# A hybrid decoder layer on one core: TensorE's order planned by another rule, true transposes, paired doubling, and two column groups at the end

## The chip, the cores and the metric

The kernel runs on one core of one Trainium2 chip. The metric is the device time of one execution in microseconds (us); lower is better. Engines are called as the profile calls them: PE is TensorE (PEld its weight loads), DVE is VectorE, ACT is ScalarE, POOL is GpSimd, SP is SyncE, which here only issues DMAs.

## What is computed

One layer over 560 tokens (16 learned tokens and 512 of a prompt in one sequence, 32 of eight short sequences), width 1024, all in fp32:

```python
h = rms_norm(x, g_mix)
proj = h @ w_in
glu_a, glu_b, qkv, z, b_raw, a_raw, gate_c, gate_d = jnp.split(proj, cuts, axis=-1)
c = jax.nn.silu(layer_norm(depthwise31(glu_a * sigmoid(glu_b)) + b_dw, ln_g, ln_b))
q, k, v = jnp.split(jax.nn.silu(depthwise4(qkv)), 3, axis=-1)    # heads of 128, q and k l2-normalised
g = -jnp.exp(a_log) * softplus(a_raw + dt_bias)                  # decay per token and head
o, S_new = gated_delta(q, k, v, sigmoid(b_raw), g, S0)           # 8 heads
o = rms_norm(o, g_head) * jax.nn.silu(z)
x = x + (sigmoid(gate_c) * (c @ w_cout) + sigmoid(gate_d) * (o @ w_dout)) @ w_o
x = x + jnp.square(jax.nn.relu(rms_norm(x, g_mlp) @ w_up)) @ w_down
y = rms_norm(x, g_final)
```

The gated delta rule is evaluated in chunks: within a chunk a triangular system is solved, and the state S (128x128 per head) is carried from chunk to chunk, S <- decay * S + k^T u, with o = (q S) * decay + (masked q k^T) u.

## The kernel before, in words

Every large matrix product is made of three products of rounded parts: weight high part by input high part, weight high by input low, weight low by input high. `gemm` goes through 88 chunks of weights (1024 x 128 each), called by their index here: 0 to 7 are those of k, 64 to 71 those of gate_c, 80 to 87 those of w_o. A chunk takes 48 matmuls at L613, called mains: for each of 8 input slices two with the high and two with the low input part (mains 0 to 31 of the chunk), and then 16 with the weight's low part. Below, mains are numbered from the first of chunk 0, so that chunk 3 is mains 144 to 191. Chunks 0 to 3 (NRAW = 4) run on the input before its norm, whose high parts lie in the tiles V2 to V9, one for each slice, and whose low parts lie in RT; chunks from 4 on run on the normalised h in tile R1. After `gemm` comes the MLP (L2083 up, L2234 down), whose matmuls are mains too.

Between the mains stand small matmuls of other streams:

- `g_stage` makes the decays: L681, L685 and L687 on PE, exponentials on ACT, then two products on POOL (L706, tiles zs0 and zs1), which PE reads in L710, L711 and L712.
- `d_gm` makes for each of the 8 heads two products on POOL (L739, a 128x512 mask times the decays). They are written to V4 to V9 in turn, three heads in six tiles, so the first six of them overwrite what the mains of chunk 3 read. `d_stage` reads them on PE (L755 to L760).
- `doubling` (L1108, L1119: 64 matmuls of 64x64) is the last step of the triangular solve.
- `head_prep` turns v, k and q of a head's short sequences (L1411, L1413, L1415, L1419) and its k (L1452), and makes the masked q k^T (L1469). `chain` walks a head's chunks: L1503 reads the state, L1518 makes u, L1522 and L1525 use it, L1537 copies o on ACT. `decode_state` writes the states of the short sequences, `head_post` norms o (L1660, L1669).
- The end: `ev_part` adds the last product to x, `mean_of` sums the squares of a group of token columns (L2282), `fin_part` adds eps (L2334, DVE), takes the power -0.5 (L2336, POOL), broadcasts it (L2340, PE), scales (L2350, L2346, DVE) and writes out (L2353). `warm` (L300) issues matmuls whose result nobody reads.

What order all this has is decided when the program is built. `Weaver` is a list scheduler: each stream yields the next operation with its engine, an assumed cost and what it depends on. The scheduler always emits the operation that can start earliest by its own books. Ties go by the stream's priority. The engines then run each its own list in that order, and waits are on semaphores. So a wait at the head of an engine's list holds up everything behind it. One line matters for the prediction: in `d_gm` the start is booked as

```python
t = E("g").t
yield wait(("mm", NRAW - 1))
```

so the books take the time of g alone, and not the end of chunk 3's mains, though the semaphores make POOL wait for the readers of V4 to V9.

## Time and profile before

| | before |
|---|---|
| median of 3 runs | 1069.06 us (1068.16 to 1070.02) |
| the profiled execution's own time | 1068.65 us |
| its span in the profile | 1066.9 us |
| PE busy | 1048.2 us, 98% |
| DVE, ACT, POOL busy | 769.4, 622.9, 148.1 us |

The span is the time between the first and the last instruction of the core; some 1.75 us of the profiled execution's time lie outside it. Busy times of PE are modelled from pipelined matmuls, so the distance from one start to the next is the better measure of what a matmul costs.

### The profile page before, as it was taken

What the parts mean: (1) busy time and instruction counts of PE and PEld (TensorE: products, weight loads), DVE (VectorE), ACT (ScalarE), POOL (GpSimd) and SP (SyncE); (2) the same over time, 40 slices, a digit from 0 to 9 for tenths busy, and PEclk for the clock granted to TensorE, in tenths of its full rate; (3) what the DMA queues carried; (4) which work ended last, traced back from release to release, by engine and by line L of the source; (5) the groups of instructions that cost most, each with busy time, mean ns of one, the idle gap of its engine ahead of it and who ended that gap; (6) DMA issues with size and microseconds to landing.
All of it is one profiled execution on the core that took longest, in us unless ns stands there. A gap on an engine that the chain in (4) does not pass through costs nothing.

```text
span 1066.9 us, 21819 instructions
## 1 busy us (share of the span) xinstructions
PE 1048.2 (98%) x8835; PEld 1026.1 (96%) x8835; DVE 769.4 (72%) x1360; ACT 622.9 (58%) x1285; POOL 148.1 (14%) x173
## 2 busy tenths in 40 slices
PE   8999999999999999999999999999999999999997
PEld 6988999999999999899999999999999999999996
DVE  5888879788889887788953355778657547746754
ACT  5677334668787878776358424578327426723741
POOL 2067311102211221122111000000000000000000
PEclk9999999999999999999999999999999999999998
DMA  6232687467576566667877522654365365346222
GB/s 213 82 89 70 124 178 164 87 148 161 139 172 164 143 137 156 164 166 182 187 163 158 179 84 91 163 153 117 109 177 129 100 153 149 94 124 164 80 61 84
DMA packets 57872, 145.55 MB, mean 136 GB/s; under 512 B 14612, under 2 KB 20140, under 8 KB 57772
## 3 DMA queue, kind: packets, MB, share of 16 engines
q1 hardware_dynamic: 46828, 104.32, 30.4%
q0 software_dynamic: 10944, 39.85, 23.2%
q8 instruction: 69, 1.13, 0.4%
q14 instruction: 31, 0.25, 0.1%
HBM read 135.14 MB, written 9.01 MB: 135 GB/s over the span
## 4 chain that ended last, share of the span: by engine, by line
PE 87%; DVE 5%; ACT 3%; DMA 3%; issue 2%; SPq 0%; POOL 0%; POOLq 0%; DVEq 0%; ACTq 0%
PE pg L613 42%; PE pg L2234 17%; PE bk L2083 15%; DVE acc L815 1%; DMA pre<-in_sq_dram 1%; DVE V L1217 1%; PE pg L2083 1%; PE bk L1419 1%; PE bk L1518 1%; PE bk L978 1%; DVE of L815 1%; PE bk L1522 1%; PE bk L1503 1%; DMA M<-in_xT_dram 1%; PE bk L1525 1%
## 5 line engine op out<-in xcount | busy, mean ns | idle before, releaser
L613 PE MATMUL pg<-R,wh 128*128 128x280 f32 (+2 forms) x1920 | 279.3, 295 | 1.0 <-ACT pre L803 1.0
L613 PEld LDWEIGHTS pg<-R,wh 128*128 128x128 f32 x1920 | 253.7, 189 | 3.9 <-issue 1.5
L1217 DVE SCALAR_TENSOR_TENSOR V<-V,vec,V 128x512 f32<-128x512 f32 x240 | 180.5, 781 | 2.2
L568 ACT ACTIVATE wh<-wraw 128x1024 fp32r<-128x1024 f32 (+1 forms) x89 | 93.4, 1049 | 94.3 <-PE pg L613 79.3
L613 PE MATMUL pg<-R,wl 128*128 128x280 f32 (+2 forms) x960 | 144.0, 294 | 0.3 <-issue 0.3
L613 PEld LDWEIGHTS pg<-R,wl 128*128 128x128 f32 x960 | 128.5, 189 | 1.8 <-issue 1.4
L581 POOL DMA_DIRECT2D wl<-in_w_dram x60 | 52.6, 876 | 343.8 <-ACT wl L579 252.5
L2014 ACT ACTIVATE whm<-RT 128x512 fp32r<-128x512 f32 x73 | 45.2, 625 | 53.0 <-PE pg L2234 34.8
L579 ACT ACTIVATE wl<-wh 128x1024 fp32r<-128x1024 f32 x60 | 63.5, 1058 | 14.8 <-PE pg L613 12.9
L1969 POOL DMA_DIRECT2D RT<-in_wu_dram x16 | 13.8, 865 | 381.6 <-DMA RT<-in_wu_dram 185.6
L2017 DVE TENSOR_TENSOR wlm<-RT,whm 128x512 fp32r<-128x512 f32 x73 | 49.8, 687 | 16.9 <-issue 8.4
L2234 PE MATMUL pg<-RD,whm 128*128 128x272 f32 (+2 forms) x272 | 57.7, 288 | 0.0
L2234 PE MATMUL pg<-K,whm 128*128 128x272 f32 (+2 forms) x272 | 57.6, 288 | 0.0
L2083 PE MATMUL bk<-R,whm 128*128 128x272 f32 x318 | 54.5, 288 | 0.0
L613 PE MATMUL pg<-K,wh 128*128 128x272 f32 x256 | 53.0, 289 | 0.2 <-DVE K L1766 0.2
L613 PE MATMUL pg<-RD,wh 128*128 128x272 f32 x256 | 53.2, 289 | 0.0
L2234 PE MATMUL pg<-RD,M 128*128 128x272 f32 x264 | 46.2, 288 | 0.0
L2014 ACT ACTIVATE whm<-wrawm 128x512 fp32r<-128x512 f32 x43 | 26.7, 623 | 32.6 <-PE pg L2234 29.7
L2083 PEld LDWEIGHTS bk<-R,whm 128*128 128x128 f32 x318 | 45.6, 189 | 0.0
L585 DVE TENSOR_TENSOR wl<-wraw,wh 128x1024 fp32r<-128x1024 f32 x28 | 35.1, 1253 | 13.5 <-ACT wh L568 9.5
L2234 PE MATMUL pg<-RD,wlm 128*128 128x272 f32 (+2 forms) x272 | 43.5, 289 | 0.0
L2234 PEld LDWEIGHTS pg<-K,whm 128*128 128x128 f32 x272 | 43.5, 188 | 0.0
(524 smaller groups left out, 2442.5 us busy)
## 6 DMA issues: line engine op xcount, KB each, us to landing
wraw<-in_w_dram SPq DMA_DIRECT2D x87, 512.0 KB, 3.8
wl<-in_w_dram POOLq DMA_DIRECT2D x60, 512.0 KB, 5.6
RT<-in_wu_dram SPq DMA_DIRECT2D x24, 512.0 KB, 5.2
RT<-in_wu_dram POOLq DMA_DIRECT2D x16, 512.0 KB, 7.3
wrawm<-in_wn_dram SPq DMA_DIRECT2D x16, 512.0 KB, 3.6
RT<-in_wn_dram SPq DMA_DIRECT2D x16, 512.0 KB, 3.5
M<-in_sd_dram SPq DMA_DIRECT2D x16, 256.0 KB, 3.4
out_osd_dram<-M SPq DMA_DIRECT2D x16, 256.0 KB, 3.8
```

The costliest lines, as they stand in the source:

```text
L568: nc.scalar.activation(wh[:, c[0]:c[1]], w[:, c[0]:c[1]], AF.Copy)
L579: nc.scalar.activation(wl, wh.bitcast(F32), AF.Copy, scale=-1.0)
L581: nc.gpsimd.dma_start(wl, i["w"][n].bitcast(F32R), accum_op=ALU.add)
L585: nc.vector.tensor_tensor(wl, w, wh.bitcast(F32), op=ALU.subtract)
L613: nc.tensor.matmul(pt[:, hf, 0:N], w[idx][:, k, :], x[:, off + hf * N:off + hf * N + N], start=k == 0 and not part and x is hi, stop=k == ...
L815: nc.vector.scalar_tensor_tensor(acc[:, 0:584], pr[:, q:q + 584], vcol(w + q), acc[:, 0:584], op0=ALU.mult, op1=ALU.add)
L1217: nc.vector.scalar_tensor_tensor(cc[:, 0:512], G[r][:, 16 + q:528 + q], vcol(w + q), cc[:, 0:512], op0=ALU.mult, op1=ALU.add)
L1969: nc.gpsimd.dma_start(rb, i["wu"][g][:, 1024:2048], accum_op=ALU.add)
L2014: nc.scalar.activation(hi, raw, AF.Copy)
L2017: nc.vector.tensor_tensor(lo, raw, hi.bitcast(F32), op=ALU.subtract)
L2083: nc.tensor.matmul(acc[an], w[:, kp, :], x, start=kp == 0 and not part and x is hi and m not in (3, 6, 7), stop=kp == 3 and part == 1, ski ...
L2234: nc.tensor.matmul(out, w[:, k % 4, :], x[:, a], start=n_ == 0 and x is hi, stop=n_ == len(STEPS) - 1)
```

## The change

The instructions keep their meaning; what changes is order, the form of some small matmuls, and the end. Lines after the change are 9 to 27 higher than before it (L739 is L748, L706 is L715, L710 is L719, L613 is L622, L1108 is L1119, L1119 is L1124, L2350 is L2377).

- The scheduler: an operation on PE is ranked by its start, its priority and its age alone. Mains are marked, and one that follows a small matmul is booked 0.09 us longer. All of PE's order is planned anew by this.
- Low parts of chunks 64 to 71: subtracted on DVE (as for chunks 0 to 11) and no longer by ACT and an accumulating DMA of POOL.
- Doubling: the second half's first step and the first half's second step go in pairs of matmuls on different quarters of the array.
- `head_prep`: v4 and, for seven heads, k4 are turned by PE's transpose and not by a product with the identity; so is o's last slice in `head_post`. The factor s moves from the masked q k^T and from kd into the copy of u on ACT, so the four DVE operations per head that made `at` become one of 128x512, and `sk` is not made. The stream `chain` is started after it.
- `chain`: the two halves of the PSUM bank that hold k S and u change places every other chunk.
- `decode_state` has a higher priority; a reciprocal of the MLP's norm waits for an earlier product.
- The end: the second part's 240 columns are two groups of 120 (before: three of 80); 8 matmuls of `warm` run while POOL takes the power; the scale by g_final of the last slice is done on ACT, so its product is a plain one on DVE; the first part's last three products and their DMAs wait until the second part's eps is added.

```diff
+                if eng == "pe":
+                    key, switch = (start, s[0], s[1]), False
+                    if best is None or key < best[0]:
+                        best = (key, s, eng, start, cost + (0.09 if self.small and tab == "main" else 0.0), tab)
+                    continue
...
-        A0, A1 = 12, 72
+        A0, A1 = 12, 64
...
-            for m in range(32):
-                t = yield op("pe", 0.058, tn[m // 16], tb)
+            def first(m, cost):
+                tb_[m // 8] = yield op("pe", cost, tn[m // 16], tb)
                 nc.tensor.matmul(B[m // 8][64:128, m % 8, :], KT[0:64, m, 64:128], Tn[0:64, m, :], start=True, stop=True)
...
+            def second(m, cost):
+                q = m // 8
+                tb_[q] = yield op("pe", cost, t1[q], *tc_[2 * (m // 16):2 * (m // 16) + 2])
+                nc.tensor.matmul(B[q][0:64, m % 8, :], P2[m // 16][64:128, m % 16, :], CTT[64:128, m, 64:128],
                                  start=True, stop=True)
...
+            for q in (2, 3):
+                for m in range(8 * q, 8 * q + 8):
+                    yield from first(m, 0.07)
+                    yield from second(m - 16, 0.07)
+                yield from keep(q)
+                yield from done(q - 2)
...
-            nc.tensor.matmul(b4[:96, 0:128], M2["v4"], ident, start=True, stop=True)
...
+            nc.tensor.transpose(b4[:96, 0:128], M2["v4"], ident)
+            yield op("pe", 0.12 if wk > 64 else 0.22, tv, tb4)
+            if wk > 64:
+                nc.tensor.transpose(b4[:wk, 128:256], k4, ident)
...
+            nc.vector.tensor_tensor(at, b.rearrange("p (t c) -> p t c", c=128), Ds[hh], op=ALU.mult)
...
+                ba, bu = (bx[:, 256:384], bx[:, 0:128]) if j % 2 else (bx[:, 0:128], bx[:, 256:384])
                 if j:
-                    t = yield op("pe", 0.22, ts, to)
-                    nc.tensor.matmul(bx[:, 0:128], ks, S, start=True, stop=True)
+                    t = yield op("pe", 0.22, ts)
+                    nc.tensor.matmul(ba, ks, S, start=True, stop=True)
...
-                nc.scalar.activation(u, bx[:, 256:384], AF.Copy)
+                nc.scalar.activation(u, bu, AF.Copy, scale=st["s"][:, hh, j:j + 1])
...
-            W.spawn(decode_state(hh, tu), 1)
+            W.spawn(decode_state(hh, tu), -2)
...
-            nc.tensor.matmul(b4[:, 0:48], ob[:, 4, :], ident[:, 0:48], start=True, stop=True)
+            t4 = yield op("pe", 0.12, t1, tb4)
+            nc.tensor.transpose(b4[:, 0:128], ob[:, 4, :], ident)
...
-        NQ = (76, 80)
+        NQ = (76, 120)
...
+            E(("eps", hf)).set(t)
+            if hf:
+                W.spawn(warm(NPOW), -4)
...
+                if c == 5 and hf == 0:
+                    yield wait(("eps", 1))
```

Two places in the new order. The first is POOL's list at the decays, before and after, from the first L739 (now L748) on; V4 to V9, zs0 and zs1 are the tiles written, the second operand gives the decays.

```order
L739 TENSOR_TENSOR V4_89_785<-cst_1_68,st_gh_19_86 128x512
L739 TENSOR_TENSOR V5_90_786<-cst_1_68,st_gl_9_76 128x512
L739 TENSOR_TENSOR V6_93_820<-cst_1_68,st_gh_19_86 128x512
L739 TENSOR_TENSOR V7_94_821<-cst_1_68,st_gl_9_76 128x512
L706 TENSOR_TENSOR zs0_98_883<-cst_1_68,st_gh_19_86 128x384
L706 TENSOR_TENSOR zs1_99_884<-cst_1_68,st_gl_9_76 128x384
L739 TENSOR_TENSOR V8_95_865<-cst_1_68,st_gh_19_86 128x512
```

```order
L748 TENSOR_TENSOR V4_68_573<-cst_1_68,st_gh_19_86 128x512
L748 TENSOR_TENSOR V5_69_574<-cst_1_68,st_gl_9_76 128x512
L748 TENSOR_TENSOR V6_70_577<-cst_1_68,st_gh_19_86 128x512
L748 TENSOR_TENSOR V7_71_578<-cst_1_68,st_gl_9_76 128x512
L748 TENSOR_TENSOR V8_72_582<-cst_1_68,st_gh_19_86 128x512
L748 TENSOR_TENSOR V9_73_583<-cst_1_68,st_gl_9_76 128x512
L715 TENSOR_TENSOR zs0_75_619<-cst_1_68,st_gh_19_86 128x384
L715 TENSOR_TENSOR zs1_76_620<-cst_1_68,st_gl_9_76 128x384
```

Four products of `d_gm` stood ahead of the pair that L710 waits for, and six stand there now. The second list is PE's around the readers of that pair (pg is the output of a main, its number that of the chunk; wh and wl are high and low weights): before, and then after from the low-part mains of chunk 3 on.

```order
L613 MATMUL pg6_709<-R1_29_97,wl6_627 128x280 x2
L613 MATMUL pg7_816<-R1_29_97,wh7_676 128x280 x32
L613 MATMUL pg7_816<-R1_29_97,wl7_717 128x280 x16
L710 MATMUL bk1_97_882<-zs0_98_883,crr_3_70 128x384
L711 MATMUL bk1_97_882<-zs1_99_884,crr_3_70 128x384
L712 MATMUL bk1_97_882<-crr_3_70 128x384
L613 MATMUL pg8_910<-R1_29_97,wh8_774 128x280 x16
L755 MATMUL bk3_104_942<-V4_89_785,crr_3_70 128x512
```

```order
L622 MATMUL pg3_493<-V4_41_181,wl3_421 128x280 x2
L622 MATMUL pg3_493<-V5_42_195,wl3_421 128x280 x2
L622 MATMUL pg3_493<-V6_44_205,wl3_421 128x280 x2
L622 MATMUL pg3_493<-V7_45_217,wl3_421 128x280 x2
L622 MATMUL pg3_493<-V8_46_231,wl3_421 128x280 x2
L622 MATMUL pg3_493<-V9_47_244,wl3_421 128x280 x2
L622 MATMUL pg4_572<-R1_29_97,wh4_468 128x280 x28
L719 MATMUL bk0_74_618<-zs0_75_619,crr_3_70 128x384
L720 MATMUL bk0_74_618<-zs1_76_620,crr_3_70 128x384
L721 MATMUL bk0_74_618<-crr_3_70 128x384
L622 MATMUL pg4_572<-R1_29_97,wh4_468 128x280 x4
L622 MATMUL pg4_572<-R1_29_97,wl4_492 128x280 x16
```

The readers of zs0 and zs1 stood behind main 383, the last of chunk 7; they now stand in chunk 4, behind main 219. L681 to L687 moved likewise, from mains 326 to 335 to mains 166 to 175. The first reader of the new V4 (L755) moved from main 400 to main 308.

The other place is the doubling on PE: a part of the first step of the second half, before (in runs of 8) and now (in pairs with the second step of the first half).

```order
L1108 MATMUL bk3_155_2339<-M_83_751 64x64 x8
L1108 MATMUL bk0_156_2340<-M_83_751 64x64 x8
L1108 MATMUL bk1_157_2341<-M_83_751 64x64 x8
L1108 MATMUL bk2_158_2342<-M_83_751 64x64 x8
L613 MATMUL pg23_2349<-R1_29_97,wh23_2082 128x280 x12
L1119 MATMUL bk3_155_2339<-RT_82_750,M_83_751 64x64 x8
```

```order
L622 MATMUL pg23_2236<-R1_29_97,wh23_2077 128x280 x18
L1119 MATMUL bk3_157_2367<-M_94_790 64x64 x8
L622 MATMUL pg23_2236<-R1_29_97,wh23_2077 128x280 x2
L1119 MATMUL bk0_158_2368<-M_94_790 64x64 x8
L622 MATMUL pg23_2236<-R1_29_97,wh23_2077 128x280 x2
L1119 MATMUL bk1_159_2369<-M_94_790 64x64
L1124 MATMUL bk3_157_2367<-RT_93_789,M_94_790 64x64
L1119 MATMUL bk1_159_2369<-M_94_790 64x64
L1124 MATMUL bk3_157_2367<-RT_93_789,M_94_790 64x64
```

Sixteen such pairs stand in two groups of eight. The first 16 of the first step and the last 16 of the second step still run alone, in runs of eight with mains between.

## Rows read from the trace of the kernel before

**Rows 1.** The page: busy time of engines, chain that ended last, group of line 585.
```profile
PE 1048.2 (98%) x8835; PEld 1026.1 (96%) x8835; DVE 769.4 (72%) x1360; ACT 622.9 (58%) x1285; POOL 148.1 (14%) x173
...
PE 87%; DVE 5%; ACT 3%; DMA 3%; issue 2%; SPq 0%; POOL 0%; POOLq 0%; DVEq 0%; ACTq 0%
...
L585 DVE TENSOR_TENSOR wl<-wraw,wh 128x1024 fp32r<-128x1024 f32 x28 | 35.1, 1253 | 13.5 <-ACT wh L568 9.5
```

**Rows 2.** Waits of TensorE, dearest lines: total us, times, longest.
```profile
PE bk L1503 <- ACT M L1537: 2.1, 2, 1.5
...
PE pg L613 <- ACT pre L803: 1.0, 1, 1.0
...
PE bk L755 <- ACT D L715: 0.8, 1, 0.8
...
PE bk L755 <- ACT RD L764: 0.6, 1, 0.6
```

**Rows 3.** Line 739 on GpSimd by form: minimum, median, maximum in ns.
```profile
L739 POOL TENSOR_TENSOR V<-cst,st_gh x8: 1035/1524/2237, 58.4 to 92.0; 128x512 fp32r<-128x512 f32 x8
L739 POOL TENSOR_TENSOR V<-cst,st_gl x8: 1035/1562/2027, 60.6 to 93.5; 128x512 fp32r<-128x512 f32 x8
```

**Rows 4.** Timeline of GpSimd, 36 to 92 us: start, length, instruction, idle before.
```profile
58.41 2.24 POOL L739 TENSOR_TENSOR V<-cst,st_gh 128x512 fp32r<-128x512 f32 x1 [36.60 <-ACT st_gh L666]
...
64.14 1.37 POOL L706 TENSOR_TENSOR zs<-cst,st_gh 128x384 fp32r<-128x384 f32 x1
```

**Rows 5.** Timeline of TensorE at weight 3 and around L681.
```profile
40.60 0.41 PE L613 MATMUL pg<-RT,wh 128*128 128x280 f32 x2
...
41.89 2.21 PE L613 MATMUL pg<-V,wl 128*128 128x280 f32 x16
43.95 4.26 PE L613 MATMUL pg<-R,wh 128*128 128x280 f32 x32
...
61.21 0.30 PE L681 MATMUL bk<-st_g,cst 128*128 128x32 f32 x2
...
64.30 0.94 PE L613 MATMUL pg<-R,wh 128*128 128x280 f32 x6
```

**Rows 6.** Windows: busy by engine, then granted clock, DMA share, GB/s.
```profile
9.00:10.00 1.00, 0.00 (x0) 0.00 (x0) 1.00 (x2) 1.00 (x3) 0.54 (x1) 1.00 1.03 397
12.00:14.00 2.00, 2.00 (x15) 1.19 (x14) 2.00 (x3) 1.99 (x4) 1.08 (x1) 0.50 1.05 406
222.00:226.00 4.00, 2.47 (x21) 2.25 (x20) 1.76 (x4) 2.38 (x6) 0.86 (x1) 1.00 0.30 111
```

**Rows 7.** Timeline of TensorE, 206 to 210 us, small matmuls of head_prep.
```profile
206.00 0.38 PE L1411 MATMUL bk<-cst,M 128*96 128x128 f32 x2
206.22 0.38 PE L1413 MATMUL bk<-cst,kq 128*96 128x128 f32 x2
...
209.48 0.60 PE L1452 MATMUL bk<-cst,M 128*128 128x128 f32 x4
209.84 0.50 PE L613 MATMUL pg<-R,wh 128*128 128x274 f32 x2
```

**Rows 8.** Timeline of TensorE in the doubling steps of `solve`.
```profile
178.71 0.19 PE L1075 MATMUL bk<-M 32*32 32x32 f32 x1
178.73 0.19 PE L1077 MATMUL bk<-M 32*32 32x32 f32 x1
178.74 0.19 PE L1075 MATMUL bk<-M 32*32 32x32 f32 x1
...
190.23 3.94 PE L1108 MATMUL bk<-M 64*64 64x64 f32 x64
```

**Rows 9.** Timeline of all engines at the end.
```profile
1057.44 0.57 PE L2282 MATMUL bk<-misc,zs 128*80 128x1 f32 x6
...
1059.25 1.41 PE L2340 MATMUL bk<-cst,ncol 80*128 80x80 f32 x6 [1.25 <-POOL ncol L2336]
...
1062.91 0.46 DVE L2346 SCALAR_TENSOR_TENSOR R<-V,vec,bk 128x240 f32<-128x240 f32 x1
```

More of the change, by code (lines that the diff above doesn't have):

```diff
@@ L119, in __init__ @@
         self.tab = None
+        self.small = False
         self.patience = 0.0
@@ L170, in run @@
             _, s, eng, start, cost, tab = best
-            if tab is not None:
+            if eng == "pe":
+                self.small = tab != "main"
+            elif tab is not None:
                 self.tab = tab
@@ L1105, in doubling, with keep, done @@
             tb = max(x[2] for x in bks)
-            for m in range(32):
-                t = yield op("pe", 0.058, tn[m // 16], tb)
+            t1, tb_ = [None] * 4, [None] * 4
+            def first(m, cost):
+                tb_[m // 8] = yield op("pe", cost, tn[m // 16], tb)
                 nc.tensor.matmul(B[m // 8][64:128, m % 8, :], KT[0:64, m, 64:128], Tn[0:64, m, :], start=True, stop=True)
-                if m % 8 == 7:
-                    tb_.append(t)
-            t1 = []
-            for q in range(4):
-                t1.append((yield from move(("act", "dve")[q % 2], 512, tb_[q], P2[q // 2][64:128, 8 * (q % 2):8 * (q % 2) + 8, :],
-                                           B[q][64:128])))
-            tb_ = []
-            for m in range(32):
-                h2 = m // 16
-                t = yield op("pe", 0.058, *t1[2 * h2:2 * h2 + 2], *tc_[2 * h2:2 * h2 + 2])
-                nc.tensor.matmul(B[m // 8][0:64, m % 8, :], P2[m // 16][64:128, m % 16, :], CTT[64:128, m, 64:128],
+            def second(m, cost):
+                q = m // 8
+                tb_[q] = yield op("pe", cost, t1[q], *tc_[2 * (m // 16):2 * (m // 16) + 2])
+                nc.tensor.matmul(B[q][0:64, m % 8, :], P2[m // 16][64:128, m % 16, :], CTT[64:128, m, 64:128],
                                  start=True, stop=True)
-                if m % 8 == 7:
-                    tb_.append(t)
-            for q in range(4):
+            def keep(q):
+                t1[q] = yield from move(("act", "dve")[q % 2], 512, tb_[q], P2[q // 2][64:128, 8 * (q % 2):8 * (q % 2) + 8, :],
+                                        B[q][64:128])
+            def done(q):
                 t = yield from move(("act", "dve")[q % 2], 512, tb_[q], CTT[0:64, 8 * q:8 * q + 8, 64:128], B[q][0:64], -1.0)
@@ L1127, in doubling @@
                     E(("dbl", hh)).set(t)
+            for q in (0, 1):
+                for m in range(8 * q, 8 * q + 8):
+                    yield from first(m, 0.116)
+                yield from keep(q)
+            for q in (2, 3):
+                for m in range(8 * q, 8 * q + 8):
+                    yield from first(m, 0.07)
+                    yield from second(m - 16, 0.07)
+                yield from keep(q)
+                yield from done(q - 2)
+            for q in (2, 3):
+                for m in range(8 * q, 8 * q + 8):
+                    yield from second(m, 0.116)
+                yield from done(q)
         def solve4(t):
@@ L1409, in head_prep @@
             b4, kb4, tb4 = yield from get_bank()
[L1410 to L1413 removed]
+            yield op("pe", 0.12, tv, tb4)
+            nc.tensor.transpose(b4[:96, 0:128], M2["v4"], ident)
+            yield op("pe", 0.12 if wk > 64 else 0.22, tv, tb4)
+            if wk > 64:
+                nc.tensor.transpose(b4[:wk, 128:256], k4, ident)
+            else:
+                nc.tensor.matmul(b4[:wk, 128:256], k4, ident, start=True, stop=True)
             yield op("pe", 0.22, tq, tb4)
@@ L1470, in head_prep @@
                                  q[:, 128 * j:128 * j + 128], start=True, stop=True)
-            for j in range(4):
-                t1 = yield op("dve", 0.263, t)
-                nc.vector.scalar_tensor_tensor(at[:, j, :], b[:, 128 * j:128 * j + 128], st["s"][:, hh, j:j + 1],
-                                               Ds[hh][:, j, :], op0=ALU.mult, op1=ALU.mult)
-                E(("at", hh, j)).set(t1)
-                if j == 0:
-                    E(("ready", hh)).set(max(t1, tx))
-                    W.spawn(chain(hh), -1)
+            t1 = yield op("dve", dve_c(512), t)
+            nc.vector.tensor_tensor(at, b.rearrange("p (t c) -> p t c", c=128), Ds[hh], op=ALU.mult)
+            E(("at", hh)).set(t1)
             put_bank(kb, t1)
+            E(("ready", hh)).set(max(t1, tx))
+            W.spawn(chain(hh), -1)
         def chain(hh):
@@ L1516, in chain @@
                     t, t2 = tr, 0.0
-                t = yield op("pe", 0.3, t, t2, tr, tbx)
-                nc.tensor.matmul(bx[:, 256:384], CT["T"][:, 4 * hh + j, :], rr, start=True, stop=True)
+                t = yield op("pe", 0.3, t, t2, to, tr, tbx)
+                nc.tensor.matmul(bu, CT["T"][:, 4 * hh + j, :], rr, start=True, stop=True)
                 tu = yield op("act", 0.17, t)
-                nc.scalar.activation(u, bx[:, 256:384], AF.Copy)
+                nc.scalar.activation(u, bu, AF.Copy, scale=st["s"][:, hh, j:j + 1])
                 t = yield op("pe", 0.22, tu)
                 nc.tensor.matmul(bx[:, 384:512], kd[:, j, :], u, start=True, stop=True)
-                ta = yield wait(("at", hh, j))
+                ta = yield wait(("at", hh))
                 to = yield op("pe", 0.22, tu, ta)
-                nc.tensor.matmul(bx[:, 0:128], at[:, j, :], u, start=True, stop=True)
+                nc.tensor.matmul(ba, at[:, j, :], u, start=True, stop=True)
                 Sn = Sb[j % 2]
@@ L1885, in mlp_norm @@
             evac_done(n, t)
-            yield wait(("upm", 4, 4))
+            yield wait(("upm", 3, 2))
             for q in range(4):
@@ L2231, in dn_product @@
                 for w, x in ((wl, hi),) if part else ((wh, hi), (wh, lo)):
-                    t = yield op("pe", sum(a.stop - a.start for _, a in parts) * 0.4605e-3, tp, tk, tf)
+                    t = yield op("pe", sum(a.stop - a.start for _, a in parts) * 0.4605e-3, tp, tk, tf, tab="main")
                     for out, a in parts:
```

49 lines of the change are left out of this document (19 added, 30 removed).

## The prediction

> **What bounds the kernel now.** I read the page first: TensorE (PE) is busy for 1048.2 us, 98% of the span, and 87% of the chain that ended last are its own [rows 1]. So the kernel gets faster where PE issues less or waits less, and slower where PE waits more; work on DVE, ACT and POOL costs only where PE stands still for it. Next the list of waits of PE. It is short: the dearest line is L1503, the first matmul of a chunk in `chain`, with 2.1 us in two waits, and three waits around the decays cost 1.0, 0.8 and 0.6 us [rows 2]. The rest of the kernel's idle PE time is at the start and the end. With so little to win in any one place, the change is a sum of small gains against whatever its new order adds, and I look for the latter with the lists of order beside the timeline.
>
> **The decays, where the new order puts a wait.** L710 needs zs0 and zs1 from POOL. It stood behind main 383 and now stands behind main 219, and POOL now makes six products of L739 before that pair, not four. Those six overwrite V4 to V9, which chunk 3's low-part mains read last (V4 at mains 180 and 181, V9 at mains 190 and 191). So when POOL starts is no longer set by g but by PE.
>
> When is PE where? Main 166 starts at 40.60 us, and a main takes 0.129 us: sixteen of them lie between the starts 41.89 and 43.95 [rows 5]. From there the new order adds the small matmuls L681 to L687; from the first of them to the main behind the last it took 3.09 us with ten mains between them, 1.29 us, so they cost 1.8 us [rows 5]. Main 181 is then done at 40.60 + 1.8 + 16 x 0.129 = 44.5 us, and POOL can start. Main 219 is done at 40.60 + 1.8 + 54 x 0.129 = 49.4 us, and PE comes to L710. g itself is not late: the operations that make it now stand ahead of chunk 4's and 5's on DVE and ACT.
>
> When is POOL done? A product of L739 takes between 1.035 and 2.24 us, with medians of 1.52 and 1.56 [rows 3]; one of L706 took 1.37 [rows 4]. Six at 1.5 and two at 1.37 are 11.7 us: POOL is done at 56.2 us. PE waits 56.2 - 49.4 = 6.8 us, and everything on PE is queued behind it, all mains of chunk 4 and after. With every product at the minimum the wait is 4.1 us, with every one at 2.0 it is 9.9 us. The last parts of h, which DVE now makes later (it still has three products of L464 to do at that time), may hold PE for half a microsecond before main 219; that lies inside the same wait. What is late next: D4's exponential stands on ACT ahead of the high part of chunk 6, which PE needs 68 mains, 8.8 us, after the wait; one exponential and one rounding fit in that.
>
> An idle of this length can also lower the clock. At the start PE did nothing between 9 and 10 us, and in 12 to 14 us the granted clock was 0.50, the lower of the two levels (1.2 GHz), which alone lost 1.0 us; the 1.5 us idle within 222 to 226 us left it at 1.00 [rows 6]. The new idle is longer than either. I take 1.5 us for it, between 0 and 2.5. The loss is 6.8 + 1.5 = 8.3 us.
>
> What this move removes are the three old waits of 1.0, 0.8 and 0.6 us [rows 2], since POOL and ACT are far ahead of PE for the rest of the decays. A stream that is pushed back may meet PE elsewhere; I take 1.5 of 2.4 us, between 0 and 2.4.
>
> **Transposes.** A product with the identity of 128x128 fp32 goes in two passes and takes 0.22 us from start to start; four transposes took 0.36 us, 0.09 each [rows 7]. Fifteen times 0.13 is 1.95 us. In `head_post` a 48-column product in two passes becomes a transpose of 128 columns, for which I take 0.05 us each, eight times 0.4. Sum 2.35, and as all of it is PE's own time it comes whole (2.0 to 2.4). The Trainium skill speaks against this in "TensorE: Matmul & The Clock Gate", section "Part 4: PE-mode transpose": about 275 ns for such a transpose within a kernel, which does not count as activity for the clock. By that figure the fifteen would cost 0.8 us more than before; this trace's 0.09 us decides.
>
> **Doubling.** L1108's 64 passes take 3.94 us, 0.062 each, so a matmul takes 0.123 [rows 8]. Whether two 64x64 matmuls on different quarters run beside each other is not shown; the nearest row is the smaller step, where 32x32 matmuls of L1075 and L1077 start 0.01 to 0.02 us apart [rows 8]. If the second is hidden, sixteen pairs save 16 x 0.123 = 2.0 us, if not, nothing. I take 1.4 less 0.2 for two more changes between mains and small ones: 1.2, between -0.2 and 1.8.
>
> **The chains.** L1503 waited for L1537's copy of o, because both used one part of the bank; with two parts that go in turn it no longer does. That removes 2.1 us [rows 2]. What is late next in a chain is L1518's operand, which DVE makes after L1503; the new order has less cover between L1522 and the next L1503, so I take 1.5, between -0.5 and 2.1. The new order also has seven runs of mains fewer in the chains, 0.09 us for each change (the step from L1452's last to the main behind it [rows 7]): 0.6 us, between 0 and 0.9. `s` in the copy of u, one DVE product for four and no `sk` take work from DVE, which doesn't bound PE; I cost them at nothing. The same holds for eight more low parts on DVE in gate_c's chunks: such a subtraction on DVE takes 1.25 us [rows 1], and PE takes 48 x 0.129 = 6.2 us for a chunk, which covers it. If that cover were gone, each would hold PE for up to 1.25 us.
>
> **The end.** Two groups of columns instead of three take four passes from L2282 after the last operand comes, 0.095 each [rows 9], of which I count 0.3. L2340 took 1.41 us for six passes [rows 9]: four at the same pace are 0.94, and less if the eight matmuls of `warm` keep the clock up while POOL works, so I take 0.7 saved (0.5 to 0.9). These eight end before POOL's power, since PE waits 1.25 us for it [rows 9]. The last product, 0.46 us [rows 9], becomes a plain one like its neighbours, 0.13 less. The three held products of the first part fit into the wait for POOL and L2340, and their DMAs are on SP before the first of the second part. Sum 1.15, between 0.7 and 1.3.
>
> **The sum.** Gains: 2.35 + 1.2 + 1.5 + 0.6 + 1.5 + 1.15 = 8.3 us. Loss: 8.3 us. So the profiled execution's 1068.65 us stay 1068.65, and against the median, which is 0.4 us above it, that is 1069.06; I say 1069.2. About 0.2%, 2.1 us, is what a measurement of this kernel can tell from no change.
>
> **Rivals.**
> - *Faster: POOL is quicker, or the clock stays.* The minimum in [rows 3] is what a product takes when POOL is undisturbed. If DVE runs dry during PE's wait, the six go at 1.1: the loss is 4.5 us, without a fall of the clock, and the gains are whole: 1068.65 + 4.5 - 8.3 = 1064.9, and about 1065.2 in the median. It decides when a product takes under 1.3 us on the mean and the clock does not fall. For it: half of the products shown were faster than 1.56. Against it: DVE has the last of h and then a row of products ahead of it at that time.
> - *Slower: POOL and DVE shut each other out.* The first L739 beside DVE took 2.24 us [rows 4], over twice the minimum. If all six take 2.0, the wait is 9.9 us, with the clock 11.7, and the sum is 1068.65 + 11.7 - 8.3 = 1072.1, 1072.5 in the median. It decides from 1.8 us on the mean. Against it stand the medians. The Trainium skill's rule is of this kind ("SBUF — State Buffer", section "Who interferes with whom": a DVE operation with two operands in SBUF and a POOL operation that reads SBUF exclude each other for a whole instruction). The spread of [rows 3] agrees with it, but not that each product meets a DVE one.
> - *The new forms save nothing.* If pairs don't run beside each other and the chains only exchange one wait for another, the gains are 5.5 us: 1068.65 + 8.3 - 5.5 = 1071.5. For it: no row shows such a pair; against it: [rows 8] for the smaller ones.
>
> **How the numbers follow.** I give 0.45 to the forecast, 0.27 to the faster case, 0.20 to the slower one, 0.08 to the last. Of the forecast's 0.45, 0.40 lies within 0.2%, 0.03 below and 0.02 above. With 0.27 that is 0.30 for faster, with 0.28 it is 0.30 for slower, and 0.40 for no difference. The range goes from 1064.3, where the faster case has its gains whole and the transposes' upper bound with it, to 1073.3, where the slower one has the clock's upper bound; one in ten is left out at each end. The forecast's own range is 1067 to 1071.5.
>
> **What the profile after would show.** A wait of PE for POOL (L719 on L715) of 5 to 9 us at about 49 us, the largest of all, with a granted clock below 1.00 right behind it. No wait of L1503's successor for the copy of o. Transposes about 0.09 us apart, pairs of the doubling about 0.13 us apart. At the end four passes of L2340's successor in about 0.7 us. The prediction is wrong if that wait is under 4 us, if the clock is low much longer than 3 us, or if the planned order makes PE wait for weights or h in places that I did not list.

## The result, and the profile after

The changed kernel takes 1082.38 us (median of 4 runs, 1081.45 to 1084.49) and the kernel before 1069.45 us beside it: a ratio of 1.0123, 95% interval 1.0107 to 1.0140, 13 us slower. The forecast was 1069.2 us, with a range up to 1073.3.

The page of the changed kernel, its span, busy time and chain, answers to [rows 1]:

```profile
span 1081.2 us, 21740 instructions
PE 1054.8 (98%) x8814; PEld 1029.0 (95%) x8814; DVE 772.4 (71%) x1343; ACT 621.3 (57%) x1280; POOL 141.2 (13%) x165
...
PE 84%; issue 4%; DMA 4%; ACT 3%; DVE 3%; POOL 2%; SPq 0%; POOLq 0%; DVEq 0%; ACTq 0%
```

The span is 14.3 us longer and PE is busy for only 6.6 us more. In the chain, PE's share has fallen from 87% to 84%, and "issue" and DMA have risen to 4% each. The waits of PE, the dearest lines, answer to [rows 2]:

```profile
PE bk L719 <- POOL zs L715: 3.2, 1, 3.2
PE bk L1542 <- ACT M L1536: 3.0, 2, 2.7
PE bk L1099 <- issue: 1.7, 1, 1.7
PE pg L2258 <- DVE V L2274: 1.7, 1, 1.7
PE pg L622 <- DVE R L473: 1.6, 2, 0.9
...
PE bk L720 <- POOL zs L715: 0.6, 1, 0.6
```

None of the three waits around the decays in [rows 2] is left, nor L1503's (now L1527) for the copy of o. Others stand there.

To place them in time I compared when ACT starts to round the high part of a chunk (L568, now L577), since PE's release of the one two chunks earlier sets it. Chunk 23's starts at 176.23 us before and 181.19 after, 5.0 us later; chunk 59's at 504.59 and 517.36, 12.8 later; chunk 87's 12.7 later; the end comes 14.3 later. So 5 us are lost up to chunk 23, 7.8 in the solve and the chains, 1.6 in the MLP and the end. The trace of the kernel before has a fall of the clock at its start that the changed kernel's has not (1.7 us, below), so up to chunk 23 the new order lost more than the 5 us.

**The decays.** Timeline of POOL, the eight products (answers to [rows 4]), and then the timeline of PE at that place:

```profile
43.78 1.04 POOL L748 TENSOR_TENSOR V<-cst,st_gh 128x512 fp32r<-128x512 f32 x1 [22.93 <-DVE M L399]
44.78 1.04 POOL L748 TENSOR_TENSOR V<-cst,st_gl 128x512 fp32r<-128x512 f32 x1
45.78 2.09 POOL L748 TENSOR_TENSOR V<-cst,st_gh 128x512 fp32r<-128x512 f32 x1
...
50.92 1.54 POOL L748 TENSOR_TENSOR V<-cst,st_gl 128x512 fp32r<-128x512 f32 x1
52.41 1.36 POOL L715 TENSOR_TENSOR zs<-cst,st_gh 128x384 fp32r<-128x384 f32 x1
53.74 1.36 POOL L715 TENSOR_TENSOR zs<-cst,st_gl 128x384 fp32r<-128x384 f32 x1
```

```profile
48.61 0.78 PE L622 MATMUL pg<-R,wh 128*128 128x280 f32 x4 [0.86 <-DVE R L473]
50.11 0.52 PE L622 MATMUL pg<-R,wh 128*128 128x280 f32 x2 [0.72 <-DVE R L473]
53.83 0.69 PE L719 MATMUL bk<-zs,crr 128*128 128x384 f32 x1 [3.20 <-POOL zs L715]
55.15 0.69 PE L720 MATMUL bk<-zs,crr 128*128 128x384 f32 x1 [0.64 <-POOL zs L715]
```

POOL starts at 43.78 us, about when PE has read V4 for the last time, and is done at 55.10. PE stops four times: 0.86 and 0.72 us for the last parts of h, 3.20 and 0.64 for POOL, 5.4 us in sum. Windows of 1 us at that place and in the solve show the clock (the third number from the end):

```profile
51.00:52.00 1.00, 0.00 (x0) 0.00 (x0) 1.00 (x2) 0.00 (x0) 1.00 (x1) 1.00 0.00 0
53.00:54.00 1.00, 0.17 (x1) 0.17 (x1) 1.00 (x2) 0.00 (x0) 1.00 (x2) 0.50 0.00 0
57.00:58.00 1.00, 1.00 (x6) 1.00 (x5) 0.94 (x2) 0.82 (x1) 0.00 (x0) 0.50 0.00 0
60.00:61.00 1.00, 1.00 (x10) 1.00 (x9) 0.57 (x1) 1.00 (x6) 0.00 (x0) 1.00 0.00 0
195.00:196.00 1.00, 0.00 (x0) 0.00 (x0) 0.28 (x1) 0.59 (x1) 0.00 (x0) 1.00 0.94 82
197.00:198.00 1.00, 1.00 (x5) 1.00 (x6) 0.39 (x1) 0.58 (x1) 0.00 (x0) 0.50 1.09 217
208.00:209.00 1.00, 1.00 (x15) 0.88 (x12) 1.00 (x3) 0.29 (x1) 0.00 (x0) 0.50 0.00 0
211.00:212.00 1.00, 1.00 (x32) 0.88 (x32) 0.00 (x0) 0.15 (x1) 0.00 (x0) 1.00 0.52 41
```

It is 0.50 from 53 to 59 us and, a second time, from 197 to 209 us; with the windows in which it changes that is 6.8 and 13.7 us. Busy time times the missing share of the clock, summed over such windows, is 2.6 us at the first place and 6.6 at the second, 9.2 in sum. Before, the clock fell only at the start (1.7 us) and at the end (0.5). So the lower clock took 6.9 us more than before, about as much as the 6.6 us by which PE is busy longer; the other 7.7 of the 14.3 us are time in which PE is idle.

**The solve.** Ahead of the second fall, among 32x32 matmuls that follow each other at a distance of 0.01 us, PE stops for 1.7 us with nothing in the trace to wait for:

```profile
194.61 0.19 PE L1097 MATMUL bk<-RT,M 32*32 32x32 f32 x1
196.48 0.20 PE L1099 MATMUL bk<-RT,M 32*32 32x32 f32 x1 [1.68 <-issue]
```

In the window 194 to 195 us the queue that the profile calls instruction carries one packet, and weights keep the DMA engines busy from 195 on (a DMA share of 0.94).

```profile
q8 instruction: 1, 0.02, 5.5%
```

This packet begins at 194.05 us and takes 0.88 (5.5% of 16 engines in 1 us); PE goes on 1.6 us after its end. The kernel before has the same block of 192 matmuls from 184.56 to 186.59 us, with no main inside either. There the packet begins at 186.47 us, 0.1 us before the block's last matmul, and PE stops behind it for 0.32 us only, among mains:

```profile
188.86 0.94 PE L613 MATMUL pg<-R,wl 128*128 128x280 f32 x6 [0.32 <-issue]
```

**The chains.** The longest wait there, 2.73 us, can be followed back to SP's queue. The load for the next short convolution (L790) stands behind an output of a state (L1658) that is not ready; ACT waits 3.04 us for the load (L812), and what the chain needs of ACT comes behind it:

```profile
299.75 0.38 SPq L1658 DMA_DIRECT2D out_osd_dram<-M  x1
300.18 0.42 SPq L790 DMA_DIRECT2D pre<-in_sq_dram  x1
...
304.64 0.20 ACT L812 ACTIVATE pre<-pg 128x32 f32<-128x32 f32 x1 [3.04 <-DMA pre<-in_sq_dram]
...
306.36 0.49 PE L1542 MATMUL bk<-M,RT 128*128 128x128 f32 x2 [2.73 <-ACT M L1536]
```

**What went as forecast.** Transposes of `head_prep` follow each other after 0.11 us, pairs of the doubling after 0.06 us for each pass of both, so 0.12 a pair, and the end's broadcast takes 0.70 us with four passes where six took 1.41 [rows 7 to 9]. A part of the latter is the clock: it was 0.73 from 1059 to 1060 us and 0.50 to 1061 in the kernel before, and is 1.00 from 1074 to 1075 now.

```profile
221.19 0.27 PE L1434 MATMUL bk<-cst,M 128*96 128x128 f32 x1
221.30 0.27 PE L1437 MATMUL bk<-cst,kq 128*96 128x128 f32 x1
```

```profile
211.34 0.22 PE L1119 MATMUL bk<-M 64*64 64x64 f32 x1
211.35 0.22 PE L1124 MATMUL bk<-RT,M 64*64 64x64 f32 x1
211.40 0.22 PE L1119 MATMUL bk<-M 64*64 64x64 f32 x1
```

```profile
1074.30 0.70 PE L2368 MATMUL bk<-cst,ncol 120*128 120x120 f32 x4 [0.21 <-POOL ncol L2364]
1075.04 2.60 DVE L2377 TENSOR_TENSOR R<-V,bk 128x240 f32<-128x240 f32 x8 [0.44 <-PE bk L2368]
```

### The profile page after: what moved, and what is told of

The parts are those of the page before. It is cut to its first block, busy times and chain, and to the rows that moved or that the text cites. A ratio compares the mean times of both kernels' runs of the same rounds, so it can differ in the third digit from the quotient of the medians.

```text
span 1081.2 us, 21740 instructions
## 1 busy us (share of the span) xinstructions
PE 1054.8 (98%) x8814; PEld 1029.0 (95%) x8814; DVE 772.4 (71%) x1343; ACT 621.3 (57%) x1280; POOL 141.2 (13%) x165
## 4 chain that ended last, share of the span: by engine, by line
PE 84%; issue 4%; DMA 4%; ACT 3%; DVE 3%; POOL 2%; SPq 0%; POOLq 0%; DVEq 0%; ACTq 0%
PE pg L622 43%; PE pg L2258 17%; PE bk L2107 14%; DMA M<-in_sd_dram 1%; POOL V L748 1%; DMA pre<-in_sq_dram 1%; PE bk L987 1%; PE bk L1494 1%; DMA out_osd_dram<-M 1%; DMA RT<-in_wu_dram 1%; PE bk L1119 1%; PE bk L1546 1%; POOL um L1640 1%; PE bk L1542 1%; PE bk L1549 0%
## 5 line engine op out<-in xcount | busy, mean ns | idle before, releaser
L622 PE MATMUL pg<-R,wh 128*128 128x280 f32 (+2 forms) x1920 | 283.1, 297 | 1.7 <-DVE R L473 1.6
L622 PEld LDWEIGHTS pg<-R,wh 128*128 128x128 f32 x1920 | 256.8, 191 | 5.6 <-DVE R L473 2.0
L1240 DVE SCALAR_TENSOR_TENSOR V<-V,vec,V 128x512 f32<-128x512 f32 x240 | 173.3, 750 | 3.4 <-ACT V L1231 1.1
L577 ACT ACTIVATE wh<-wraw 128x1024 fp32r<-128x1024 f32 (+1 forms) x89 | 93.4, 1050 | 106.2 <-PE pg L622 97.4
L622 PE MATMUL pg<-R,wl 128*128 128x280 f32 (+2 forms) x960 | 144.1, 296 | 0.0
L622 PEld LDWEIGHTS pg<-R,wl 128*128 128x128 f32 x960 | 129.5, 191 | 0.8 <-issue 0.6
L590 POOL DMA_DIRECT2D wl<-in_w_dram x52 | 45.6, 877 | 342.8 <-ACT wl L588 265.5
L594 DVE TENSOR_TENSOR wl<-wraw,wh 128x1024 fp32r<-128x1024 f32 x36 | 44.7, 1242 | 36.7 <-PE pg L622 21.5
L588 ACT ACTIVATE wl<-wh 128x1024 fp32r<-128x1024 f32 x52 | 55.1, 1060 | 12.9 <-PE pg L622 10.2
L2258 PE MATMUL pg<-RD,whm 128*128 128x272 f32 (+2 forms) x272 | 57.7, 288 | 1.7 <-DVE V L2274 1.7
L2258 PE MATMUL pg<-K,whm 128*128 128x272 f32 (+2 forms) x272 | 57.7, 288 | 0.0
L2107 PE MATMUL bk<-R,whm 128*128 128x272 f32 x318 | 54.4, 288 | 0.0
L622 PE MATMUL pg<-K,wh 128*128 128x272 f32 x256 | 53.2, 289 | 0.2 <-DVE K L1790 0.2
L622 PE MATMUL pg<-RD,wh 128*128 128x272 f32 x256 | 53.0, 288 | 0.0
L2258 PE MATMUL pg<-RD,M 128*128 128x272 f32 x264 | 46.2, 288 | 0.0
L2107 PEld LDWEIGHTS bk<-R,whm 128*128 128x128 f32 x318 | 45.5, 188 | 0.0
L2258 PEld LDWEIGHTS pg<-RD,whm 128*128 128x128 f32 x272 | 43.4, 188 | 1.9 <-issue 1.9
L2258 PE MATMUL pg<-RD,wlm 128*128 128x272 f32 (+2 forms) x272 | 43.4, 288 | 0.0
```

Of the source, the lines that this page charges most:

```text
L577: nc.scalar.activation(wh[:, c[0]:c[1]], w[:, c[0]:c[1]], AF.Copy)
L588: nc.scalar.activation(wl, wh.bitcast(F32), AF.Copy, scale=-1.0)
L590: nc.gpsimd.dma_start(wl, i["w"][n].bitcast(F32R), accum_op=ALU.add)
L594: nc.vector.tensor_tensor(wl, w, wh.bitcast(F32), op=ALU.subtract)
L622: nc.tensor.matmul(pt[:, hf, 0:N], w[idx][:, k, :], x[:, off + hf * N:off + hf * N + N], start=k == 0 and not part and x is hi, stop=k == ...
L1240: nc.vector.scalar_tensor_tensor(cc[:, 0:512], G[r][:, 16 + q:528 + q], vcol(w + q), cc[:, 0:512], op0=ALU.mult, op1=ALU.add)
```

## The experiments

All ratios are to the kernel before on the same chip; single executions of it there took 1066.0 to 1074.5 us.

| run | median us | ratio | 95% interval |
|---|---|---|---|
| after | 1082.38 | 1.0123 | 1.0107 to 1.0140 |
| c1_book | 1085.38 | 1.0144 | 1.0127 to 1.0160 |
| c2_no009 | 1065.47 | 0.9964 | 0.9946 to 0.9981 |
| a4_oldkey | 1062.97 | 0.9930 | 0.9906 to 0.9954 |
| a4_again | 1064.69 | 0.9956 | 0.9940 to 0.9972 |
| a1_books | 1080.02 | 1.0120 | 1.0064 to 1.0176 |
| c3_no24 | 1074.80 | 1.0044 | 1.0028 to 1.0061 |
| f1_gap | 1077.73 | 1.0079 | 1.0060 to 1.0098 |
| h1_both | 1074.20 | 1.0052 | 1.0026 to 1.0078 |
| b1_pairs | 1067.50 | 0.9980 | 0.9964 to 0.9997 |
| b3_transp | 1066.32 | 0.9956 | 0.9939 to 0.9972 |
| b2_tail | 1067.62 | 0.9990 | 0.9974 to 1.0006 |
| b4_chain | 1072.71 | 1.0030 | 1.0016 to 1.0044 |
| a2_prio | 1081.02 | 1.0100 | 1.0073 to 1.0127 |
| g1_best | 1073.26 | 1.0030 | 1.0013 to 1.0048 |

The theory after the result: the new order of PE, not the new forms of its matmuls, costs the time, at three kinds of places (the decays, the stop in the solve, the chains). The rival: the moved and paired small matmuls are dear themselves.

### The order: old rank, and the booking alone

a4_oldkey takes both parts of the scheduler's change back and keeps everything else; a4_again is the same file.

```diff
-                    key, switch = (start, s[0], s[1]), False
+                    key, switch = (start + (self.patience if s[0] == 4 else 0.6 if s[0] == 2.5 else 0.0), s[0], s[1]), False
...
-                        best = (key, s, eng, start, cost + (0.09 if self.small and tab == "main" else 0.0), tab)
+                        best = (key, s, eng, start, cost, tab)
```

> The changed kernel with PE's old rank (patience kept, no 0.09 us for a main behind a small matmul). Theory (the new rank, not the new forms of matmuls, costs the time): the readers of the pair stand behind main 383 again, no wait over 2 us before 100 us, and the time is 1064 to 1068 us, or 1072 to 1075 if a fall of the clock near the doubling comes with the new forms. Rival (pairs and transposes cost it): 1078 us or more.

> The run with the old rank and booking once more, beside the others on one chip: 1061 to 1065 us.

1062.97 us, a little below the expected 1064 to 1068, and 1064.69 us: 18 to 19 us faster than the changed kernel. L690 stands at mains 326 to 330 again and L719 behind main 383. Windows over the decays and the solve:

```profile
40.00:100.00 60.00, 57.60 (x462) 54.23 (x461) 49.77 (x62) 46.04 (x101) 31.55 (x22) 1.00 0.27 78
175.00:215.00 40.00, 39.33 (x661) 37.39 (x660) 32.30 (x48) 23.20 (x44) 4.70 (x17) 1.00 0.53 114
```

The clock is 1.00 in both; in the changed kernel it is 0.94 and 0.83 in the same windows.

c1_book is the reverse, the scheduler's change on the kernel before, every instruction in its old form:

```diff
+                if eng == "pe":
+                    key, switch = (start, s[0], s[1]), False
+                    if best is None or key < best[0]:
+                        best = (key, s, eng, start, cost + (0.09 if self.small and tab == "main" else 0.0), tab)
+                    continue
```

> The kernel before with the scheduler's part of the change alone: PE's new rank and 0.09 us more in the books for a main behind a small matmul; every instruction is as before, in another order. Theory (this booking moves the decays forward into chunks 3 and 4, and all that was lost follows from it): a wait of 4 to 7 us near 50 us with the clock at 0.50 behind it, and 1077 to 1089 us in all. Rival (the loss needs the new forms as well): within 3 us of the kernel before.

1085.38 us, more than the whole change and within the theory's range. Its list of waits has the wait for POOL, a little under the expected 4 to 7 us, and the stop in the solve (also 2.4 us for weights near 596 us, a place that the changed kernel has not):

```profile
PE bk L719 <- POOL zs L715: 3.2, 1, 3.2
...
PE bk L1099 <- issue: 1.9, 1, 1.9
```

c2_no009 parts the two: the changed kernel with only the 0.09 us taken out.

```diff
-                        best = (key, s, eng, start, cost + (0.09 if self.small and tab == "main" else 0.0), tab)
+                        best = (key, s, eng, start, cost + 0.0, tab)
```

> The changed kernel with one number changed: nothing is booked for a main behind a small matmul. Its order up to the MLP is that of the run with the old rank. Theory (the 0.09 us alone moves the decays): 1061 to 1065 us, faster than both kernels, with no wait near 50 us and no stop near 195 us. Rival (dropping the patience in the rank also costs): 1067 us or more.

1065.47 us, a little above the expected 1065. Its order up to the MLP is a4_oldkey's. So the 0.09 us in the books is what moves the decays and costs 17 us; what the new rank without it costs is within the noise (0.9964 against 0.9956 for a4_again), though it brings one wait of 1.7 us in the MLP (L2258 for L2274, as in the changed kernel). Why a booking this small brings the decays ahead by 160 mains was not followed through the books.

### The decays

a1_books books `d_gm` from the end of chunk 3's mains:

```diff
-                t = E("g").t
-                yield wait(("mm", NRAW - 1))
+                t = max(E("g").t, (yield wait(("mm", NRAW - 1))))
```

> The changed kernel, but the products for V4 to V9 are booked from the end of chunk 3's mains, so only two of them stand ahead of the pair that PE waits for near 50 us. Theory (six products of 1.4 us each ahead of that pair cost the wait and the fall of the clock behind it): the wait near 50 us falls from 5.4 to under 2 us, the granted clock stays 1.00 there, and the whole is 5 to 8 us faster than the changed kernel, 1074 to 1077 us, if the fall of the clock near 196 us comes back. Rival (the moved small matmuls themselves cost the time): 1080 to 1083 us.

Two products stand ahead of the pair now, and PE comes to L719 with nothing to wait for:

```profile
45.84 1.90 POOL L715 TENSOR_TENSOR zs<-cst,st_gh 128x384 fp32r<-128x384 f32 x1
47.70 1.43 POOL L715 TENSOR_TENSOR zs<-cst,st_gl 128x384 fp32r<-128x384 f32 x1
...
50.41 0.34 PE L719 MATMUL bk<-zs,crr 128*128 128x384 f32 x1
```

At chunk 23 it is 3.3 us ahead of the changed kernel, and the clock near 50 us is 1.00. The mechanism is as expected, but the whole is not: the median lies in the rival's range, single runs were 1077.8, 1082.2, 1089.4 and 1077.8 us, and the interval overlaps that of the changed kernel. That this mend alone makes the kernel faster is not shown. The stop in the solve is there again (2.3 us), and the clock low behind it for 6.8 us between 192 and 200 us.

### The stop in the solve

The first theory was that a transfer of weights delays the instructions. c3_no24 takes away the accumulating DMA that ran at that time:

```diff
-                if A0 <= n < A1:
+                if A0 <= n < A1 and n != 24:
```

> The changed kernel, but the low part of chunk 24 is subtracted on DVE, so that the accumulating DMA that was under way when TensorE stopped at 194.8 us is not made. Theory (TensorE's instructions came late because that transfer held the DMA engines, and the stop let the clock fall for 13 us): no stop over 1 us at the smallest matmuls of the solve, clock 1.00 there, 1073 to 1077 us. Rival (the stop has another cause, such as the density of the instructions alone): a stop of 1.5 us or more again and 1080 to 1084 us.

The time is as the theory had it, the reason is not. PE stops for 2.2 us again, and the clock happens not to fall behind it:

```profile
196.00:199.00 3.00, 0.79 (x65) 0.66 (x54) 0.96 (x2) 0.90 (x2) 0.00 (x0) 1.00 0.14 55
199.00:205.00 6.00, 6.00 (x66) 5.55 (x59) 4.73 (x8) 2.83 (x4) 0.00 (x0) 1.00 0.27 82
```

So that transfer was not the cause, though the fall of the clock was the costly part. The time of c3_no24 also has its order of the chains in it and is not the price of the fall alone. f1_gap tests the density: 16 mains between the two halves of the densest matmuls.

```diff
-                    yield op("pe", 0.027, t1[q])
+                    yield op("pe", 0.027, t1[q], *([ta[0] + 2.0] if q else []))
```

> The changed kernel, but the second half of the densest small matmuls (three 32x32 for each of 16 blocks) is booked 2 us after the first, so that 16 mains stand between the halves. Theory (TensorE runs through its instructions there faster than the next block of them is brought, whatever else the DMA engines carry, and the stop of 1.7 to 2.3 us can let the clock fall): no stop over 0.6 us there, clock 1.00 from 180 to 215 us, 1072 to 1077 us. Rival (the stop has to do with what stands ahead of it, not with density): a stop of 1.5 us or more again, 1079 us or more when the clock falls for long.

1077.73 us, just above the upper end. There is no stop: PE is busy through all of 180 to 220 us, at full clock. As in c3_no24, the order of the chains behind it is another too.

```profile
180.00:220.00 40.00, 40.00 (x666) 38.07 (x665) 35.70 (x46) 21.86 (x40) 5.63 (x18) 1.00 0.55 117
```

All five orders with this block undivided in its new place stopped there (1.7 us in the changed kernel, 1.9 in c1_book, 2.3, 2.0 and 2.2 in a1_books, a2_prio and c3_no24), against 0.6 us at most around the solve in those with the old place; f1_gap and h1_both, which divide it, did not. That dividing the block ends the stop is shown. Density alone is not the cause: in the old place the same 192 matmuls stand undivided in nine traces, all within 2.0 to 2.6 us. What the stops have in common is the instruction packet. The five long ones end 1.2 to 1.6 us after the end of one, and so do all five stops over 0.3 us that the traces with the old place put down to "issue" (in the kernel before, a4_oldkey, a4_again, b4_chain and g1_best, 0.3 to 0.6 us). This speaks for instructions that come late; no run varied the packets. Why the stop is longer in the new place stays open: in the changed kernel the packet begins 0.6 us before the last matmul ahead of the stop, in the kernel before 0.1 us before the end of the block, with 12 mains behind it that go on meanwhile.

h1_both has both mends, the edits of a1_books and f1_gap.

> The changed kernel with both mends: the products for V4 to V9 booked from the end of chunk 3, and 16 mains between the halves of the densest small matmuls. Theory (two places, the pair near 50 us and the stop near 195 us, each with the clock behind it, make most of the loss): 1069 to 1073 us, clock 0.995 or more; what is still above the run with the old rank stands in the list of waits in the chains and the MLP. Rival (each mend only moves the loss to the next place): 1076 us or more.

1074.20 us, above what the theory gave and below the rival. The clock is 0.997 over the span. Chunk 87 comes 7.5 us later than in a4_again: 2.2 of it by chunk 23, the rest in the chains. Its waits (here L1526 is the changed L1527, and L2257 its L2258):

```profile
PE pg L2257 <- DVE V L2273: 1.7, 1, 1.7
...
PE bk L1526 <- DVE M L1555: 1.6, 2, 1.0
...
PE bk L1545 <- ACT M L1543: 1.5, 3, 0.7
PE bk L1644 <- POOL um L1639: 1.4, 2, 1.1
```

They are many and short. The two mends give back 8.2 of the 17.7 us between the changed kernel and a4_again; 9.5 are left. By the pages of h1_both and a4_oldkey, whose clocks are alike (0.997), 7.7 us of the difference between these two executions are idle PE time and 3.6 us longer busy time, which no run explains. Nor is every wait that of the order: a4_oldkey and a4_again are one program, and a wait at the entry to the MLP (L2107 for L2166) took 0.6 us in one trace and 2.8 in the other.

### The parts on the kernel before

b1_pairs has the new text of the doubling, b3_transp the edits of `head_prep` and `head_post` for the three transposes, b2_tail those of the end (all as in the diff of the change).

> The kernel before with the paired doubling alone. Theory (pairs run beside each other, and the clock near 200 us fell because of the 1.7 us stop ahead of it): about 0.11 us for a pair, granted clock 1.00 through the doubling, 1066.5 to 1068.5 us. Rival (pairs with mains between are what lowers the clock): a clock of 0.50 in the doubling and 1072 us or more.

> The kernel before with the transposes alone (v4, k4 for seven heads, o's last slice). As forecast: 2.0 to 2.4 us faster, transposes of head_prep 0.09 to 0.11 us apart. Rival (what PE saves comes back as waits in the chains, since each operand is ready no earlier): under 1 us faster, with as much more in the list of waits.

> The kernel before with the change of the end alone (two groups of 120 columns, eight matmuls during the power, three products held back, the last scale on ACT). As forecast: 1.15 us faster than before (0.7 to 1.3). Rival (what is saved before the last products is given back by the outputs): within 0.3 us of the kernel before.

Pairs: 0.2% faster (0.03 to 0.36), pairs run beside each other, and the clock is 1.00 through the doubling, so pairs don't lower it. Transposes: 0.44% (0.28 to 0.61), about twice what their own account gives; its trace has shorter waits too, but it is of the fastest of seven executions (1061.32 us). The end: 0.1%, an interval that has zero in it, so that theory and rival are not told apart; in the changed kernel's trace the stretch from the last addition to x (L2328, 1071.18 us) to the last product's end (1077.64) is 6.46 us, and before it is 7.24.

b4_chain lets the two halves of the chain's bank take turns, on the kernel before:

```diff
+                ba, bu = (bx[:, 256:384], bx[:, 0:128]) if j % 2 else (bx[:, 0:128], bx[:, 256:384])
...
-                    t = yield op("pe", 0.22, ts, to)
-                    nc.tensor.matmul(bx[:, 0:128], ks, S, start=True, stop=True)
+                    t = yield op("pe", 0.22, ts)
+                    nc.tensor.matmul(ba, ks, S, start=True, stop=True)
```

> The kernel before, with the two halves of the chain's bank taking turns and nothing else. As forecast: the waits of L1503 for the copy of o (2.1 us) go and the whole is 1.5 us faster, between 0.5 us slower and 2.1 us faster. Rival (the wait is exchanged for one of the next operand in the chain): within 0.4 us of before, with L1518 or L1522 in the list of waits in its place.

Slower by 0.3% (0.16 to 0.44), outside what either side expected. The wait for the copy of o is still there, one time for 1.87 us, though the matmul now writes the other half:

```profile
222.63 0.49 PE L1505 MATMUL bk<-M,K 128*128 128x128 f32 x2 [1.87 <-ACT M L1539]
```

The trace is of the fastest of twelve executions (1067.88 us, the median is 1072.71), so it does not show where the 3 us go.

g1_best takes the turns out of a4_oldkey's kernel, with the operands' times in the books as they were before:

```diff
-                ba, bu = (bx[:, 256:384], bx[:, 0:128]) if j % 2 else (bx[:, 0:128], bx[:, 256:384])
+                ba, bu = bx[:, 0:128], bx[:, 256:384]
```

> The changed kernel with PE's old rank and booking and with the chain's bank used as before (no turns). If taking turns costs time in any order, as it did alone, this is 1 to 4 us faster than the run with the old rank, 1059 to 1062 us. If it cost only through the order that it happened to bring, the two are within 1.5 us.

1073.26 us, 8.6 us slower than a4_again on the same chip; both expectations were wrong. The loss is in another place, loads of states that come late:

```profile
PE bk L1570 <- DMA M<-in_sd_dram: 7.5, 4, 3.7
```

a2_prio gives `decode_state` its old priority (`-2` becomes `1` in its spawn).

> The changed kernel with decode_state at its old priority. Theory (SP's queue stood behind an output that was not ready, so a load that ACT waited for came late, and L1542 waited 2.7 us): no wait of L1542 over 1 us, 1078 to 1081 us, the rest as in the changed kernel. Rival (that wait comes from elsewhere): 1082 to 1083 us with the wait still there.

1081.02 us, at the theory's upper end. L1542's wait of 2.7 us is gone. That fits SP's queue as its cause, but does not show it: in c3_no24, f1_gap and h1_both, which keep the new priority, L1542 waits for 0.5 us or less. Waits for loads of states rose from 0.9 to 1.7 us, and the interval overlaps that of the changed kernel.

## Why the prediction was wrong

- **The decays: right in mechanism, and in sum partly by luck.** Forecast were PE at L710's successor at 49.4 us, POOL done at 56.2, a wait of 6.8 and 1.5 for the clock, 8.3 in sum. Measured: PE there at 50.6, POOL done at 55.1, 5.4 us of waits and 2.6 for the clock: 8.0. Of the waits only 3.84 are for POOL, under the 4 us that I had named as a sign of being wrong; 1.58 are for h, which I had put inside the wait for POOL at 0.5, where they came ahead of it. The clock's 2.6 lie above my bound of 2.5, and it was low for 6.8 us, over the 3 us that I had named as another such sign. In the sum these errors cancel. The six products took 8.9 us, 1.5 each as assumed. The three old waits went, as said.
- **The step that failed is the sum: "Loss: 8.3 us".** It takes the new order's loss to stand at one place. c1_book puts the price of the order alone at 15 us. The two other parts were costed at nothing or nearly: the solve, of whose move I charged only 0.2 us for two changes between mains and small ones, and where PE stopped for 1.7 us and worked for 13.7 us at 1.2 GHz (6.6 us lost); and the chains and the MLP, for whose new order I counted a gain of 0.6 us, and which took waits of 2.7, 1.7 and 1.1 us. What the rest of the loss is made of stays open (h1_both).
- **The chains' 1.5 us: wrong.** "With two parts that go in turn it no longer does": in b4_chain it did. What keeps the wait (the trace shows only that it ends with the copy) stays open.
- **The clock.** That an idle stretch lowers it was right at 50 us: all five traces with this wait (after, c1_book, a2_prio, c3_no24, f1_gap) have the clock low there for 6.8 to 10.2 us, a1_books and h1_both, without it, have not. In the solve it fell too, which I had not counted on, and after the stops it stayed low for 13.7, 6.8, 6.8 and 3.4 us in after, a1_books, c1_book and a2_prio, and did not fall in c3_no24. The length of a stop does not settle it: a4_again's clock fell after 1.1 us of idle near 9 us, b1_pairs' stayed at 1.00 after 1.5 us at that place, and a1_books' after 2.6 us at 721 us.
- **Transposes, pairs and the end: right in mechanism.** 0.11 us a transpose, 0.12 a pair, 0.8 us at the end for a forecast of 1.15. The 275 ns of the Trainium skill ("TensorE: Matmul & The Clock Gate", section "Part 4: PE-mode transpose") are what a single record lasts here too (270 to 273 ns for L1434), but not the distance from one to the next. a4_again and a4_oldkey, the change without the new rank, are 5.0 and 6.5 us faster than the kernel before, against 5.3 us forecast for transposes, pairs, the end and the chains' runs; as the transposes alone gave about twice their forecast, that sum is no proof of its terms.
- **The rivals.** The slower one needed products of 1.8 us on the mean, and they took 1.5; its 11.7 us also count 1.8 for the clock where the forecast has 1.5. That POOL and DVE shut each other out is not refuted by this. The first two products took 1.04 us each, with DVE idle or adding from PSUM (L799); the third, begun 0.03 us after a DVE operation of 1.21 us, took 2.09, and beside the last ones DVE's three products for h took 1.24 us each, against 0.72 for one at 41.89 us, where POOL was idle:

```profile
47.83 3.73 DVE L473 TENSOR_TENSOR R<-M,R 128x560 fp32r<-128x560 f32 x3
```

The fastest version is a4_oldkey: the whole change without the two edits of the rank, 0.4 to 0.7% faster than before. b3_transp, the transposes alone, gives 0.4% too.

## What to carry to other kernels

A cost in a scheduler's books is an edit of the whole program: 0.09 us there moved a group of operations by 160 mains, and 15 us went with it. When an order is planned anew, list every place where it differs, on DMA queues too, and take the dense groups of small matmuls for places where the engine may stop. Test the rank and the new instructions apart; parts measured alone did not add up (the kernel with the chain's turns was 0.3% slower than without them in one order and 0.8% faster in another).

## What the runs showed of the hardware

- TensorE stopped for 1.7 to 2.3 us among 192 32x32 matmuls 0.01 us apart, with no semaphore to wait for, in all five orders that had them undivided in the new place, and for 0.6 us at most in nine traces that had them undivided in the old one; 16 larger matmuls between the halves ended it. All ten stops over 0.3 us that the traces put down to "issue" ended 1.2 to 1.6 us after the end of a packet on the queue that the profile calls q8 instruction.
- After such a stop the granted clock was 0.50 for between 0 and 13.7 us, with PE busy nearly all that time: in the changed kernel from 197 to 209 us, with 4.5 us of mains in a row at its beginning. Behind the 3.2 us wait at the decays it fell in five of five traces; elsewhere it fell after 1.1 us of idle in one trace and stayed at 1.00 after 2.6 in another.
- Two 64x64 matmuls on different quarters of the array took the time of one (0.12 us a pair).
